# Decode attention in two parts: scores behind their head's recurrence, values one head later

## The chip, the cores and the metric

One NeuronCore of a Trainium2 chip runs the whole program. The metric is device time in microseconds (us), the median of several executions. Five engines work side by side: PE (TensorE, matmul), DVE (VectorE), ACT (ScalarE), POOL (GpSimd) and SP (SyncE, which here only issues loads and stores). Each runs its own list of instructions strictly in order and waits at an instruction until what it needs is there.

## What is computed

One layer of a hybrid decoder step, for a prompt of 1024 rows and for 8 sample rows that each bring one new token. Three branches (A attention, B spatial gating, C gated recurrence) read one projection of the normalised input, and one output projection merges them. The part that the change touches is branch A of the sample rows ("decode"): each sample row attends over its cache with three patterns of window and stride.

```python
PATTERNS = ((128, 1), (512, 4), (2048, 16))
def _dilated_step(q, k_new, v_new, k_buf, v_buf):
    kk = jnp.concatenate([k_buf, k_new], axis=1)
    vv = jnp.concatenate([v_buf, v_new], axis=1)
...
    for win, dil in PATTERNS:
        back = jnp.arange(win // dil + 1)[None, :] * dil
        idx = jnp.clip(W + t - back, 0, W + T - 1)
        s = jnp.einsum('bthe,btnhe->bthn', q, kk[:, idx])
        p, lse = _softmax_stats(s)
        outs.append(jnp.einsum('bthn,btnhe->bthe', p, vv[:, idx]))
        lses.append(lse)
    return _combine_patterns(outs, lses)
```

Branch C, in whose stage the decode work is placed, is per head a recurrence `S = exp(g) * S + k v`, `o = q S`, computed for the prompt in blocks of 128 rows and for each sample row as one step.

## The kernel before

The program runs branch A of the prompt, then hgrn() (branch C, from about 530 to 1065 us), then sgu() (branch B) and out_proj(). hgrn() goes over six heads in three pairs hp. For a pair c_proj_i projects the values, c_proj_z the output gates (both heads); for each head c_proj_qf projects q and f. All projections go through proj groups: weights are loaded raw by SP (load_w, line 190), ACT rounds them to the fast matmul type (line 192), POOL subtracts the rounded from the raw ones to get the low part (line 193), PE multiplies both parts, and DVE or ACT takes each finished group out of PSUM. There are two PSUM banks for these groups (tag "proj"), so PE can start a group only when the group before the last has been taken out. For q and the gates DVE does that (gate(), line 152, then a multiply in line 156).

c_head(h) is the recurrence of head h on the prompt: scans and exponentials (G, eG, H), then for four pairs of blocks the scaled copies T (lines 611 to 623, DVE), small matmuls lv and ls (PE), masked copies of lv into the block matrix cmat (lines 686 to 693, DVE), matmuls po from cmat, V, eG and the state S (PE), and the next state S (line 704, DVE). c_step(h) is the step of the 8 sample rows: two loads of state ss and two of values vb, six DVE operations of 128x512 (lines 735 to 737), eight matmuls pd.

decode(h) is the sample rows' attention for heads 2h and 2h+1 of branch A: POOL clears the score tile dsc; for each half of the batch a load of q (dqb), three loads of cached keys (dk), a multiply (line 913) and a reduce (line 914) for each; then the maximum over keys (917), across partitions by two transposes on PE (pmx, pmb) with a reduce and a copy between them (921, 922), the subtraction (925), Exp on ACT, a weighting (927), a sum (928), a matmul pdn and a reciprocal (931); then six loads of cached values (dv), 24 matmuls pda, a copy and two transposes (to_columns, pdt), and three small DVE operations (941, 942) that put the result into ysT, which only out_proj reads.

The decode tiles and c_step's vb and ss share one pool of five buffers (pq), used in turn; pd, pdt, pmx, pmb, pdn and pda share one PSUM bank (tag "tr"); dsc has one buffer. The order of each engine's instructions isn't written out: a scheduler (line 1058) fixes it when the program is built, by an estimate of its own of when each instruction could run, with ties and buffers in the order of the code. So where decode stands in the code decides where its instructions are mixed in among the others.

## Time and profile before

| | |
|---|---|
| median of 3 executions | 1364.37 us (1363.49 to 1366.2) |
| profiled execution, its own time | 1367.91 us |
| its span, first to last instruction | 1366.1 us |
| mean granted clock of PE | 0.951 |
| PE busy | 1277.9 us (94%) |
| DVE busy | 914.3 us (67%) |
| ACT busy | 661.0 us (48%) |
| POOL busy | 292.6 us (21%) |

The trace is of the profiled execution, so sums from it are held against 1367.91 us. A row of the timeline gives the start in us, the duration, the engine, the line, the operation with its tiles (result<-sources) and, in square brackets, how long the engine had been idle before it and which engine's result ended that. A row of busy time by stretch gives start:end, the length, the busy time of PE, PEld (weight load), DVE, ACT and POOL with the number of records, then the granted clock, the busy share of the DMA engines and GB/s. The granted clock (PEclk) is given as a share of full speed.

### The profile page before, as it was taken

The page shows a single profiled execution, that of the slowest core. Times are in us where ns is not written, and L with a number is a line of the kernel's source. Part 1 is how long each engine was busy: PE and PEld are TensorE (multiplying, and loading weights), DVE is VectorE, ACT ScalarE, POOL GpSimd, SP SyncE. Part 2 cuts the span into 40 slices and gives each one's busy share as a digit, 9 for nine tenths or more (in the row PEclk, how much of TensorE's full clock was granted, in tenths as well). Part 3 has the DMA queues.
Part 4 walks back from the last instruction along what each step waited for, and adds up shares of the span by engine and source line. Part 5 has one row for each costly group of instructions (what it writes and reads, how often), then busy time and mean ns, then how long its engine had stood idle before and what let it go on. Part 6 is the DMA issues. An engine that isn't in the chain of part 4 may idle for free. (4 is left out here: it accounts for less than half of the span.)

```text
span 1366.1 us, 27783 instructions
## 1 busy us (share of the span) xinstructions
PE 1277.9 (94%) x10634; PEld 1160.8 (85%) x10634; DVE 914.3 (67%) x2439; ACT 661.0 (48%) x1510; POOL 292.6 (21%) x267
## 2 busy tenths in 40 slices
PE   4799999999889999999999998998899999999999
PEld 3699798779779797898888888987788899899998
DVE  5835775565774656668888988888887623654653
ACT  4435454454443554456654744545544423544543
POOL 2531210131121212112202020211111135311221
PEclk9899899889999799999999999999999999999999
DMA  6241122220221212202433243434253313612210
GB/s 220 42 141 36 47 66 70 59 68 18 58 84 58 76 36 77 65 29 67 119 97 109 90 121 115 111 97 134 61 156 96 92 32 108 207 51 81 74 46 31
DMA packets 165044, 114.23 MB, mean 84 GB/s; under 512 B 13944, under 2 KB 158864, under 8 KB 164912
## 3 DMA queue, kind: packets, MB, share of 16 engines
q1 hardware_dynamic: 157520, 110.28, 27.3%
q10 hardware_dynamic: 6816, 1.54, 0.5%
q8 instruction: 83, 1.36, 0.4%
q0 software_dynamic: 576, 0.64, 0.3%
q14 instruction: 49, 0.40, 0.1%
HBM read 84.60 MB, written 22.09 MB: 78 GB/s over the span
## 5 line engine op out<-in xcount | busy, mean ns | idle before, releaser
L100 PE MATMUL pqk<-wh_qk,h 128*128 128x256 f32 x768 | 159.6, 299 | 5.2 <-ACT h L233 2.8
L100 PE MATMUL pc<-h,wh_cqf 128*128 128x344 f32 x576 | 144.1, 332 | 4.5 <-DVE cz L152 4.5
L100 PE MATMUL po<-woh,yl 128*128 128x256 f32 x512 | 145.0, 284 | 1.9 <-POOL yl L1011 1.9
L100 PE MATMUL po<-woh,yh 128*128 128x256 f32 x512 | 145.7, 285 | 0.0
L100 PE MATMUL po<-wol,yh 128*128 128x256 f32 x512 | 144.4, 282 | 0.0
L100 PEld LDWEIGHTS pqk<-wh_qk,h 128*128 128x128 f32 x768 | 131.5, 204 | 9.8 <-ACT h L233 3.0
L100 PE MATMUL pqk<-wl_qk,h 128*128 128x256 f32 x384 | 114.0, 297 | 0.0
L100 PEld LDWEIGHTS pc<-h,wh_cqf 128*128 128x128 f32 x576 | 102.1, 194 | 7.1 <-DVE cz L152 5.0
L100 PEld LDWEIGHTS po<-woh,yh 128*128 128x128 f32 x512 | 97.1, 190 | 5.6 <-ACT yh L1010 3.9
L100 PEld LDWEIGHTS po<-woh,yl 128*128 128x128 f32 x512 | 97.2, 190 | 4.1 <-POOL yl L1011 2.4
L100 PEld LDWEIGHTS po<-wol,yh 128*128 128x128 f32 x512 | 97.3, 190 | 0.0
L100 PE MATMUL pc<-h,wl_cqf 128*128 128x344 f32 x288 | 94.9, 332 | 2.5 <-POOL wl_cqf L193 2.2
L436 DVE CUSTOM_DVE_ANT_0 s<-s,masks 128x512 f32<-128x512 f32 (+2 forms) x144 | 77.7, 584 | 13.8 <-PE s L100 13.3
L100 PE MATMUL pi<-wh_ci,h 128*128 128x256 f32 x384 | 77.6, 297 | 4.8 <-DVE dsc L925 1.9
L100 PE MATMUL pv<-wh_v,h 128*128 128x256 f32 x384 | 79.1, 297 | 1.9 <-DVE ss L165 1.6
L473 ACT ACTIVATE st<-st 128x512 f32<-128x512 f32 (+2 forms) x84 | 44.2, 536 | 72.9 <-PE st L100 70.2
L100 PEld LDWEIGHTS pqk<-wl_qk,h 128*128 128x128 f32 x384 | 78.1, 204 | 0.5
L100 PE MATMUL pcz<-h,wh_cz 128*128 128x344 f32 x288 | 71.5, 326 | 0.3 <-DVE q L152 0.3
L100 PE MATMUL paz<-h,wh_az 128*128 128x344 f32 x288 | 71.1, 329 | 0.0
L100 PEld LDWEIGHTS pi<-wh_ci,h 128*128 128x128 f32 x384 | 64.2, 201 | 6.9 <-issue 2.9
L1011 DVE TENSOR_TENSOR yl<-yb,yh 128x512 fp32r<-128x512 f32 x44 | 30.4, 692 | 58.0 <-ACT yh L1010 58.0
L100 PEld LDWEIGHTS pv<-wh_v,h 128*128 128x128 f32 x384 | 65.7, 204 | 3.0 <-ACT yo L499 1.8
(376 smaller groups left out, 3665.1 us busy)
## 6 DMA issues: line engine op xcount, KB each, us to landing
wro<-in_w_out_dram SPq DMA_DIRECT2D x32, 256.0 KB
wr_qk<-in_w_in_dram SPq DMA_DIRECT2D x48, 128.0 KB
wr_cqf<-in_w_in_dram SPq DMA_DIRECT2D x48, 128.0 KB
dk<-in_cache_k_dram SPq DMA_DIRECT2D x24, 192.0 KB
dv<-in_cache_v_dram SPq DMA_DIRECT2D x24, 192.0 KB
xt<-in_x_prompt_dram SPq DMA_DIRECT2D x8, 512.0 KB
xr<-in_x_prompt_dram SPq DMA_DIRECT2D x32, 128.0 KB
out_o_yp_dram<-xr SPq DMA_DIRECT2D x32, 128.0 KB
```

What stands on the lines that cost most here:

```text
L100: nc.tensor.matmul(out, lhsT=lhsT, rhs=rhs, start=start, stop=stop)
L436: nc.vector.tensor_tensor_reduce(out=ps[:, :w], in0=ps[:, :w], in1=nmask[:, S - n + c:S - n + c + w], op0=ALU.add, op1=ALU.max, scale=1.0, ...
L473: nc.scalar.activation(st[:, :o], st[:, :o], AF.Exp)
L1011: (nc.gpsimd if piece == 0 else nc.vector).tensor_tensor(yl[:, sl, :], y, yh[:, sl, :].bitcast(F32), ALU.subtract)
```

## The change

decode(h) is cut in two functions. decode_scores(h) does everything up to the score tile: memsets, loads of q and keys, six multiplies and six reduces. decode_values(h) does the rest. decode_scores(h) stands where decode(h) stood, behind c_step(h). decode_values(h) stands one head later, between c_head(h+1) and c_step(h+1); that of the last head stands behind the loop. Two heads' scores are therefore alive at once: the even heads keep the tile dsc, the odd heads get columns 872 to 1009 of the 1024-column tile cmat, which nothing else uses.

```diff
--- before.py
+++ after.py
@@ -753,12 +753,16 @@
                 a = c_proj_qf(2 * hp)
                 Z = c_proj_z(hp)
                 c_head(2 * hp, *a, V[0], Z[0], At, lmask, dmask)
+                if hp:
+                    decode_values(2 * hp - 1, scw)
                 c_step(2 * hp, *a)
-                decode(2 * hp)
+                scw = decode_scores(2 * hp, None)
                 a = c_proj_qf(2 * hp + 1)
                 c_head(2 * hp + 1, *a, V[1], Z[1], At, lmask, dmask)
+                decode_values(2 * hp, scw)
                 c_step(2 * hp + 1, *a)
-                decode(2 * hp + 1)
+                scw = decode_scores(2 * hp + 1, cm[:, 872:1010])
+            decode_values(5, scw)
 
             n = HC * NS
             sq = pq("ssq", (P, n))
@@ -884,35 +888,38 @@
             cns[nm] = cp.tile(list(ins[nm].shape), F32, name=nm)
             tc.keep_in_program_order(nc.scalar.dma_start(cns[nm], ins[nm]))
 
-        def decode(p):
-
-            ROWS = ((P, 1920, 1), (96, 1536, 4), (96, 0, 16))
+        ROWS = ((P, 1920, 1), (96, 1536, 4), (96, 0, 16))
+
+        def rows(cache, new, p, bb, nm):
             ch = slice(p * P, (p + 1) * P)
-
-            def dk(nm, shape=(P, 4, P)):
-                return pq(nm, shape)
-
-            def rows(cache, new, bb, nm):
-                for kind, (n, r0, step) in enumerate(ROWS):
-                    t = dk(f"{nm}{p}_{bb}_{kind}")
-                    src = cache[0].rearrange("b r h e -> r b (h e)")[r0:r0 + n * step, 4 * bb:4 * bb + 4, ch]
-                    nc.sync.dma_start(t[0:n], src[0:n * step:step])
-                    if kind == 1:
-                        nc.sync.dma_start(t[n:n + 1], new[None, 4 * bb:4 * bb + 4, ch])
-                        n += 1
-                    yield kind, n, t
-
-            scw = small(f"dsc{p}", 138, bufs=1, tag="dsc").rearrange("p (k a) -> p k a", k=3)
+            for kind, (n, r0, step) in enumerate(ROWS):
+                t = pq(f"{nm}{p}_{bb}_{kind}", (P, 4, P))
+                src = cache[0].rearrange("b r h e -> r b (h e)")[r0:r0 + n * step, 4 * bb:4 * bb + 4, ch]
+                nc.sync.dma_start(t[0:n], src[0:n * step:step])
+                if kind == 1:
+                    nc.sync.dma_start(t[n:n + 1], new[None, 4 * bb:4 * bb + 4, ch])
+                    n += 1
+                yield kind, n, t
+
+        def decode_scores(p, home):
+
+            ch = slice(p * P, (p + 1) * P)
+            scw = small(f"dsc{p}", 138, bufs=1, tag="dsc") if home is None else home
+            scw = scw.rearrange("p (k a) -> p k a", k=3)
             sc = scw[:, :, 0:16]
             nc.gpsimd.memset(sc, NEG)
             nc.gpsimd.memset(scw[:, :, 16:], 0.0)
             for bb in range(2):
-                qb = dk(f"dqb{p}_{bb}")
+                qb = pq(f"dqb{p}_{bb}", (P, 4, P))
                 nc.sync.dma_start(qb, qkv_d[0, 4 * bb:4 * bb + 4, ch].partition_broadcast(P))
-                for kind, n, t in rows(ins["cache_k"], qkv_d[1], bb, "dk"):
+                for kind, n, t in rows(ins["cache_k"], qkv_d[1], p, bb, "dk"):
                     nc.vector.tensor_tensor(t[0:n], t[0:n], qb[0:n], ALU.mult)
                     nc.vector.tensor_reduce(sc[0:n, kind, 8 * bb:8 * bb + 8], t[0:n].rearrange("p b (h e) -> p (b h) e", e=E),
                                             AX.X, ALU.add)
+            return scw
+
+        def decode_values(p, scw):
+            sc = scw[:, :, 0:16]
             mx = small(f"dmx{p}", 32, bufs=1, tag="dmx")
             nc.vector.tensor_reduce(mx[:, 0:16], sc.rearrange("p k a -> p a k"), AX.X, ALU.max)
             pt = p_dk(f"pmx{p}")
@@ -931,7 +938,7 @@
             nc.vector.reciprocal(mx[:, 16:32], pd[:, 0:16])
             pa = p_dk(f"pda{p}")
             for bb in range(2):
-                for kind, n, t in rows(ins["cache_v"], qkv_d[2], bb, "dv"):
+                for kind, n, t in rows(ins["cache_v"], qkv_d[2], p, bb, "dv"):
                     for b in range(4):
                         mm(pa[32 * b:32 * b + 32, bb * P:(bb + 1) * P], scw[0:n, kind, 8 * bb + 2 * b:8 * bb + 2 * b + 32],
                            t[0:n, b, :], kind == 0, kind == 2)
```

No instruction is added or dropped; the scheduler orders them anew. The first heads' work up to about 700 us stays as it was. Three places show what moves. (Names carry head, half and group, then a number of the tile; x4 is four in a row.)

PE, the 24 value matmuls of head 1 (pda1). Before, they follow the recurrence of their own head (lv1, ls1), ahead of the second part of the gate projection pcz1_0_0:

```order
L100 MATMUL lv1_2_7940<-T1_2_q_7937,k1_7601 32x48 x4
L100 MATMUL ls1_2_7941<-V0_1_6397,kT1_0_7822 128x128
L100 MATMUL pda1_8279<-dv1_0_0_8280,dsc1_8230 32x128 x4
L100 MATMUL pda1_8279<-dv1_0_1_8286,dsc1_8230 32x128 x4
L100 MATMUL pda1_8279<-dv1_0_2_8293,dsc1_8230 32x128 x4
L100 MATMUL pda1_8279<-dv1_1_0_8299,dsc1_8230 32x128 x4
L100 MATMUL pda1_8279<-dv1_1_1_8305,dsc1_8230 32x128 x4
L100 MATMUL pcz1_0_0_8818<-h01_81,wh_cz1_2_8804 128x344
```

After, they stand in the middle of the projection of head 3's f (pc3_1_2) and read the scores from cmat:

```order
L100 MATMUL pc3_1_2_9559<-h00_80,wl_cqf3_1_9484 128x344
L100 MATMUL pda1_9365<-dv1_0_0_9366,cmat_6353 32x128 x2
L100 MATMUL po1_1_7953<-cmat_6353,V0_1_6397 128x128
L100 MATMUL pda1_9365<-dv1_0_0_9366,cmat_6353 32x128 x2
L100 MATMUL pda1_9365<-dv1_0_1_9372,cmat_6353 32x128 x3
L100 MATMUL po1_1_7953<-eG1_7730,S1_5_8038 128x128
L100 MATMUL po1_1_7953<-cmat_6353,V0_1_6397 128x128
L100 MATMUL po1_1_7953<-eG1_7730,S1_6_8120 128x128
L100 MATMUL pda1_9365<-dv1_0_1_9372,cmat_6353 32x128
L100 MATMUL pda1_9365<-dv1_0_2_9379,cmat_6353 32x128 x4
L100 MATMUL pda1_9365<-dv1_1_0_9385,cmat_6353 32x128 x4
L100 MATMUL pda1_9365<-dv1_1_1_9391,cmat_6353 32x128 x4
```

They have moved from before the gate projection of heads 2 and 3 to behind it. DVE, around the evacuation of the gate projection (cz1_0 and cz1_1, lines 152 and 156). Before, the operations of c_step(2) on vb2 and ss2 stand between the evacuations:

```order
L735 TENSOR_TENSOR vb2_1_9426<-vb2_1_9426,qs2_8787 128x512
L941 TENSOR_TENSOR dmx1_8263<-pdt1_8320,dmx1_8263 64x8 x2
L736 TENSOR_TENSOR ss2_1_9427<-ss2_1_9427,qs2_8787 128x512
L156 TENSOR_TENSOR cz1_0_8816<-cz1_0_8816,czt1_0_1_8874 128x344
L737 TENSOR_TENSOR ss2_0_9415<-ss2_0_9415,vb2_0_9414 128x512
L942 TENSOR_TENSOR ysT_73<-ysT_73,dmx1_8263 128x8
L152 TENSOR_SCALAR cz1_0_8816<-pcz1_0_2_8880 128x344
L737 TENSOR_TENSOR ss2_1_9427<-ss2_1_9427,vb2_1_9426 128x512
L704 SCALAR_TENSOR_TENSOR S1_3_7994<-S1_2_7990,eL1_7809,ls1_2_7941 128x128
L708 SCALAR_TENSOR_TENSOR cz0_1_6848<-po1_0_7824,gn_367,cz0_1_6848 128x512
L156 TENSOR_TENSOR cz1_0_8816<-cz1_0_8816,czt1_0_2_8905 128x344
L152 TENSOR_SCALAR cz1_1_8817<-pcz1_1_0_8911 128x344
```

After, the last evacuation, that of pcz1_1_2, stands among copies T2 of head 2's recurrence:

```order
L642 TENSOR_TENSOR eG2_8943<-eG2_8943,q2_8536 128x1024
L152 TENSOR_SCALAR cz1_1_8753<-pcz1_1_1_8878 128x344
L617 TENSOR_TENSOR T2_0_0_8975<-T2_0_0_8975,q2_8536 128x192
L617 TENSOR_TENSOR T2_0_1_8984<-T2_0_1_8984,q2_8536 128x192
L686 COPY_PREDICATED cmat_6353<-cmat_6353,lv1_4_7984 128x2x2x8
L686 COPY_PREDICATED cmat_6353<-cmat_6353,lv1_6_8070 128x2x8
L152 TENSOR_SCALAR cz1_1_8753<-pcz1_1_2_8909 128x344
L932 TENSOR_TENSOR cmat_6353<-cmat_6353,pmb1_9356 128x3x16
L618 TENSOR_TENSOR T2_0_0_8975<-T2_0_0_8975,dec2_0_0_8979 128x64
```

and c_step(2) follows some 55 rows later:

```order
L735 TENSOR_TENSOR vb2_0_9413<-vb2_0_9413,qs2_8723 128x512
L686 COPY_PREDICATED cmat_6353<-cmat_6353,lv2_0_9005 128x8x2
L736 TENSOR_TENSOR ss2_0_9414<-ss2_0_9414,qs2_8723 128x512
L564 SCALAR_TENSOR_TENSOR ft3_0_9588<-k3_9506,f3_9504 128x344
L564 SCALAR_TENSOR_TENSOR ft3_1_9591<-k3_9506,f3_9504 128x344
L686 COPY_PREDICATED cmat_6353<-cmat_6353,lv2_0_9005 128x2x8x2
L702 COPY S2_0_9054<-ls2_0_9006 128x128
L735 TENSOR_TENSOR vb2_1_9425<-vb2_1_9425,qs2_8723 128x512
L737 TENSOR_TENSOR ss2_0_9414<-ss2_0_9414,vb2_0_9413 128x512
L736 TENSOR_TENSOR ss2_1_9426<-ss2_1_9426,qs2_8723 128x512
```

The six operations of c_step(2) have moved from ahead of the three evacuations of cz1_1 to behind them. PE, the second half of head 2's recurrence (po2_1). Before, it stands behind 72 matmuls of head 4's f projection (pc4_1_0 to pc4_1_2):

```order
L100 MATMUL pc4_1_2_10623<-h01_81,wh_cqf4_3_10561 128x344
L100 MATMUL pc4_1_2_10623<-h11_83,wh_cqf4_3_10561 128x344
L100 MATMUL pc4_1_2_10623<-h01_81,wl_cqf4_3_10562 128x344
L100 MATMUL po2_1_9230<-cmat_6353,V1_0_8365 128x128
L100 MATMUL po2_1_9230<-eG2_9007,S2_3_9208 128x128
L100 MATMUL po2_1_9230<-cmat_6353,V1_0_8365 128x128
L100 MATMUL po2_1_9230<-eG2_9007,S2_4_9311 128x128
L919 MATMUL pmx3_10234<-ident_65,dmx3_10232 16x128
L100 MATMUL pc4_0_0_10661<-h00_80,wh_cqf4_0_10540 128x344
```

After, it stands inside the value projection (pi2_3) that comes ahead of that f projection:

```order
L100 MATMUL pi2_3_10424<-wl_ci2_2_10243,h01_81 128x256
L723 MATMUL pdt2_10161<-ident_65,pdt2s_10159 128x128 x2
L100 MATMUL pi2_3_10424<-wh_ci2_2_10242,h11_83 128x256
L100 MATMUL pi2_3_10424<-wh_ci2_2_10242,h01_81 128x256
L100 MATMUL pi2_3_10424<-wl_ci2_2_10243,h01_81 128x256
L100 MATMUL pi2_3_10424<-wh_ci2_2_10242,h11_83 128x256
L100 MATMUL po2_1_9166<-cmat_6353,V1_0_8301 128x128
L100 MATMUL po2_1_9166<-eG2_8943,S2_3_9144 128x128
L100 MATMUL po2_1_9166<-cmat_6353,V1_0_8301 128x128
L100 MATMUL po2_1_9166<-eG2_8943,S2_4_9247 128x128
L100 MATMUL pi2_3_10424<-wh_ci2_3_10248,h01_81 128x256
```

The recurrence's matmuls now come 72 projection matmuls of 344 columns and 30 of 256 earlier in PE's list.

## Rows read from the trace of the kernel before

**Rows 1.** The page, part 1: busy us (share of span) and instructions

```profile
PE 1277.9 (94%) x10634; PEld 1160.8 (85%) x10634; DVE 914.3 (67%) x2439; ACT 661.0 (48%) x1510; POOL 292.6 (21%) x267
```

**Rows 2.** Busy time by stretch, start:end us, length, engines, PEclk, DMA

```profile
760.00:880.00 120.00, 113.17 (x1185) 105.05 (x1184) 105.05 (x314) 62.81 (x148) 20.83 (x18) 0.97 0.39 109
...
sum 420.00, PE 392.67 PEld 357.18 DVE 360.25 ACT 222.08 POOL 74.67; mean PE 98.17 PEld 89.30 DVE 90.06 ACT 55.52 POOL 18.67
```

**Rows 3.** Timeline of PE, matmuls with idle time before them

```profile
791.81 0.76 PE L100 MATMUL pc<-h,wh_cqf 128*128 128x344 f32 x2 [1.95 <-DVE cz L152]
...
822.89 0.39 PE L100 MATMUL pi<-wh_ci,h 128*128 128x256 f32 x1 [1.61 <-DVE q L152]
...
832.09 0.37 PE L100 MATMUL pdn<-dmx,ones 128*128 128x16 f32 x2 [2.44 <-DVE eL L640]
...
906.18 0.43 PE L100 MATMUL pd<-ss,qs 128*32 128x128 f32 x8 [1.45 <-DVE ss L737]
...
938.71 0.86 PE L100 MATMUL pc<-h,wh_cqf 128*128 128x344 f32 x2 [2.58 <-DVE cz L152]
...
966.72 1.05 PE L100 MATMUL pss_bv<-wr_bv,hs 128*8 128x256 f32 x16 [1.77 <-DVE q L152]
...
970.90 0.55 PE L100 MATMUL pbv<-wh_bv,h 128*128 128x256 f32 x1 [3.14 <-DVE dsc L925]
...
1010.54 0.80 PE L100 MATMUL po<-cmat,V 128*128 128x128 f32 x2 [2.20 <-DVE cmat L693]
```

**Rows 4.** Busy time by stretch, ahead of and behind gaps

```profile
783.00:791.70 8.70, 6.24 (x47) 5.02 (x45) 8.70 (x16) 4.58 (x11) 7.29 (x5) 1.00 0.33 87
791.80:795.20 3.40, 3.39 (x12) 3.39 (x13) 2.88 (x16) 1.66 (x6) 0.00 (x0) 0.54 1.06 263
832.00:836.00 4.00, 3.91 (x22) 3.94 (x23) 3.97 (x19) 0.65 (x3) 0.00 (x0) 0.63 0.02 6
938.70:942.00 3.30, 3.29 (x12) 3.29 (x13) 3.20 (x6) 0.93 (x3) 0.00 (x0) 0.52 0.78 236
970.90:976.00 5.10, 5.10 (x24) 5.10 (x25) 4.97 (x23) 4.60 (x12) 0.00 (x0) 0.50 0.24 78
1010.50:1013.50 3.00, 2.96 (x14) 2.96 (x15) 2.94 (x10) 0.00 (x0) 0.00 (x0) 0.50 0.85 276
```

**Rows 5.** Timeline of POOL in two bursts of subtractions

```profile
783.67 4.71 POOL L193 TENSOR_TENSOR wl_cqf<-wr_cqf,wh_cqf 128x512 fp32r<-128x512 f32 x2 [22.25 <-ACT wh_cqf L192]
...
788.38 2.58 POOL L193 TENSOR_TENSOR wl_cqf<-wr_cqf,wh_cqf 128x512 fp32r<-128x512 f32 x2
...
962.59 6.33 POOL L193 TENSOR_TENSOR wl_bv<-wr_bv,wh_bv 128x512 fp32r<-128x512 f32 x4 [26.51 <-ACT wh_bv L192]
```

**Rows 6.** Timeline of DVE beside those bursts and behind one

```profile
788.63 1.19 DVE L618 TENSOR_TENSOR T<-T,dec 128x64 f32<-128x64 f32 x1
789.74 1.59 DVE L156 TENSOR_TENSOR cz<-cz,czt 128x344 f32<-128x344 f32 x1
...
791.76 0.21 DVE L618 TENSOR_TENSOR T<-T,dec 128x64 f32<-128x64 f32 x1
...
967.80 2.21 DVE L566 SCALAR_TENSOR_TENSOR k<-k,lb,f 128x1032 f32<-128x1032 f32 x1
```

**Rows 7.** Timeline of DVE in a full stretch

```profile
845.53 0.69 DVE L735 TENSOR_TENSOR vb<-vb,qs 128x512 f32<-128x512 f32 x1
846.14 0.68 DVE L737 TENSOR_TENSOR ss<-ss,vb 128x512 f32<-128x512 f32 x1
```

**Rows 8.** Busy time by stretch, instructions of tile pc alone

```profile
857.00:872.20 15.20, 11.92 (x72) 11.31 (x72) 0.00 (x0) 0.91 (x2) 1.00 0.67 185
```

**Rows 9.** Timelines of DVE and PE, masked copy and first matmul of po2_1

```profile
870.00 0.37 DVE L693 COPY_PREDICATED cmat<-cmat,lv 96x192 f32<-96x192 uint16 x1
...
872.09 0.38 PE L100 MATMUL po<-cmat,V 128*128 128x128 f32 x2
```

**Rows 10.** Waits of POOL: engine line waited for, us, times, longest

```profile
POOL dsc L907 <- PE pda L100: 59.8, 3, 21.3
```

## The prediction

> **What bounds the kernel now.** I read the profile's page first, for which engine is busy, then the busy times by stretch, then the gaps ahead of TensorE's (PE's) instructions, then what VectorE (DVE) and GpSimd (POOL) did just ahead of each gap. PE is busy 94% of the span and DVE 67% [rows 1]. The change only touches the recurrence stage, and the order of PE's instructions first differs at about 700 us. From 640 to 1060 us PE is busy 392.67 of 420 us, so 27.3 us of idle time are all that a new order can win directly; DVE is busy 360.25 of the same 420, and 105.05 of the 120 us from 760 to 880 [rows 2]. DVE is not full, yet nearly always late by a little.
>
> The gaps show that. Eight that the new order can reach are 1.95, 1.61, 2.44, 1.45, 2.58, 1.77, 3.14 and 2.20 us, 17.1 us together, and each ends on a DVE result: the evacuation of a projection bank (line 152), the copy of eL (line 640), ss (737), the decode subtraction (925), the masked copy into cmat (693) [rows 3]. A gap costs twice: ahead of the 1.95 us gap the granted clock is 1.00, the 2.4 GHz level; in the stretches behind the five gaps of 1.95, 2.44, 2.58, 3.14 (with 1.77 just ahead of it) and 2.20 us it averages 0.54, 0.63, 0.52, 0.50 and 0.50, where 0.50 is the 1.2 GHz level [rows 4]. Full speed less these, times their lengths, is 1.6 + 1.5 + 1.6 + 2.6 + 1.5 = 8.7 us.
>
> Why DVE is late stands one engine further. POOL subtracts the rounded weights from the raw ones in bursts of four (line 193): two instructions from 783.67 and two from 788.38, then four from 962.59 on [rows 5]. Inside them a DVE multiply of 128x64 elements takes 1.19 us, and an add-sized one of 128x344 takes 1.59 us; the same 128x64 multiply takes 0.21 us once the burst is over, and k of head 5 takes 2.21 us [rows 6]. All of these read two tiles from SBUF. The evacuation that PE waits for sits behind such an instruction.
>
> The Trainium skill has the rule, in SBUF — State Buffer, section "Who interferes with whom": a DVE instruction with two SBUF inputs and a GpSimd instruction that reads SBUF share a pair of ports, which whichever starts first holds to its end. The trace agrees (1.19 against 0.21 us for one shape). By that rule the bursts stay as costly as they are wherever the decode steps stand, which is my second rival.
>
> **The change, part by part.** Nothing is added or taken away: the same mults, reduces, matmuls and loads run. So the sum is about who stands ahead of whom. At each gap I compare what no longer stands ahead on DVE (that much earlier is the awaited result) with what no longer stands ahead on PE (that much earlier does PE ask for it); the difference is the slack won. In a full stretch one 128x512 DVE instruction follows another after about 0.61 us, although each is recorded with 0.68 or 0.69 [rows 7], so I use 0.6.
>
> *Values one head later.* The reductions, transposes, exponential and 24 value matmuls of head h now stand behind c_head(h+1), and c_step(h+1) behind them. At the 1.95 us gap (head 3's second bank waits for the last evacuation of cz1_1), the six operations of c_step(2) (6 x 0.6 = 3.6 us), the multiply cz1_1 (1.5) and one of T2 (1.1), and ten small ones of decode 1 (0.12 to 0.17 each, 1.3) are now behind the evacuation: 7.5 us. PE loses 24 value matmuls (1.6 us), pd2's eight (0.9), and five small ones (0.7): 3.2 us. Slack won: 4.3, more than the gap. Part of the 7.5 ran ahead of moments in which DVE waited anyway; if only cz1_1 and T2 count (2.6), against the PE work that stood behind them (pd2 and its transposes, 1.3), it is 1.3, and 0.65 us of gap stays. I take the whole 1.95. The same count gives at the next gaps, in us of slack: head 2's pi2_0 +1.5 (gap 1.61, removes 1.47), pdn2 +3.2 (2.44), pd4 +11.7 (1.45; it simply stands later), pc5_1_1 +2.4 (DVE 4.7 for six operations of c_step(4) and small ones, less PE 2.3; removes 2.42 of 2.58), pss_bv0 and pbv0 +4.5 and +2.9 (the slow k5 and decode 4's steps now stand behind q5's evacuations; of 1.77 + 3.14 I count 3.03, since a delay of the first is part of the second), po4_1 +2.6 (2.20). Sum: 1.95 + 1.47 + 2.44 + 1.45 + 2.42 + 3.03 + 2.20 = **15.0 us of gaps**, and up to 8.7 of clock behind them.
>
> *Where slack is lost.* Second half of head 2's recurrence, po2_1, at 872.09 us: it waits for a masked copy that started at 870.00 and took 0.37, so it has 1.72 us to spare [rows 9]. Ahead of it PE now lacks 72 matmuls pc4 (11.9 us in their window [rows 8]), 30 of pi2 (3.7), pd3 and its transposes (1.0): 16.6 us less cover. DVE lacks there the six mults and six reduces of decode 3 (12 x 0.6 = 7.2) and c_step(3) (3.8), 0.4 of small ones: 11.4. So 16.6 - 11.4 - 1.7 = **3.5 us of new wait**, which by the pattern of [rows 4] brings some 1.5 us of half clock. A little later pcz2_0_0 waits for q4 behind 13.6 us more of head 3's recurrence; its 8.7 of slack becomes -3.3, the same lag and not paid twice.
>
> *What the saved time meets.* 5.9 us of the gaps (1.95 + 1.47 + 2.44) lie ahead of that place. If PE comes there 5.9 earlier and DVE no earlier, they are lost again. DVE idles 15 us of 760 to 880 [rows 2], mostly waiting for PE, and these shrink as PE hurries: I let half come through and charge 3.0.
>
> *Bursts on other work.* With the same bursts beside other DVE work, new small gaps open where now none are. I have no row of it; the bounds are 0 and the 15.0 that the present order pays, and I take 4.0, near the low end, because the evacuations gain 2 to 4 us of slack against multiplies stretched by about 1 us each.
>
> *Second home for scores.* Scores of heads 1, 3 and 5 go to unused columns of the mask tile, so POOL's memset need not wait for the value matmuls of the head before; in before that wait was 59.8 us in three waits [rows 10]. POOL's next subtraction waits over 20 us for ScalarE's cast anyway [rows 5], so I price it at nothing; if a subtraction did queue behind a late memset it would cost what a late lo-weight costs PE, one gap of 1.5 to 2 us.
>
> *Loads.* The key and value loads share five buffers in the same cyclic order; SP now issues weights for the coming projections ahead of c_step's and decode's loads. Only one place is tighter: the last value tile of head 3 is issued behind two weight loads and a store, and PE has 3.5 us of other work between the first and the last value matmul instead of 5.6. Bound 0 to 1 us; I take 0.
>
> **Sum.** Won 15.0 + half of 8.7 (4.3, because a stretch behind a removed gap may have a smaller one left in it) = 19.3. Lost 3.5 + 1.5 + 3.0 + 4.0 = 12.0. Net **7 us faster**. The profiled execution took 1367.91 us, 3.5 above the median of 1364.37; taken off the median, 1364.4 - 7 = **1357.4 us**.
>
> **Rivals.** *Slower: DVE's lag at head 2 to 3 decides.* For it: the 11.4 us of cover on DVE against 16.6 on PE are counted instruction by instruction, and from 760 to 1000 DVE is the engine that PE nearly always waits for. If DVE has no idle time to give back there, the 5.9 us won ahead of po2_1 come back as waits, and the 9.1 behind it too, since 13.6 us of recurrence now stand ahead of q4 and then of the banks of head 5. What is left is 3.5 + 1.5 = 5 us slower: **1369.4**. It decides as soon as DVE's idle time between 846 and 872 us cannot take up 3.5 us. Against it: the slack at the later gaps is counted too, and is positive.
>
> *No change: the gaps belong to the bursts.* POOL's bursts stay, each stretches four or so DVE instructions by about 1 us, and whichever evacuation stands behind is late: eight gaps are moved, not removed. Then the 15.0 come back elsewhere, with their clock, and the result is **1364.4 within 2.7**. For it: the gaps at 791.81, 966.72 and 970.90 of [rows 3] stand at the end of a burst or right behind one [rows 5]. Against it: what PE waits for is not the burst but the queue of DVE work ahead of the evacuation, and that queue gets 2 to 4 us shorter.
>
> *The gain is larger.* If the lag at po2_1 is covered (0) and all of the clock comes back, 15.0 + 8.7 - 4.0 - 3.0 = 16.7: **1347.7**.
>
> **How the numbers follow.** 0.2% of 1364 us, 2.7 us, is about what a measurement of this kernel can tell from no change. Chances: net gain as summed 0.42, the larger gain 0.13, bursts decide 0.23, DVE's lag decides 0.22. The first two are faster by over 0.2% except for a tail of the first; some of the bursts' case spills over to faster: faster 0.56, same 0.21, slower 0.23. The range goes from the larger gain to the slower rival's 1369.4: 1347.5 to 1369.5.
>
> **What would show it.** Right: no gap over 1 us ahead of pc of heads 3 and 5, pdn2 and pbv0; PE's idle time in the stage falls from 27 to about 18 us; a new wait of po2_1 on cmat of 2 to 4 us. Wrong: PE's idle time stays at 27 us with other names in the list; or the wait at po2_1 exceeds 5 us and banks of heads 4 and 5 wait for q; or PE waits for dv tiles (loads), which I priced at nothing.

## The result: slower, and where the time went

The changed kernel takes 1379.70 us against 1363.93 of the kernel before (medians of four executions each): a ratio of 1.0103, 95% interval 1.0085 to 1.0121. That is slower, and beyond the upper end of the predicted range (1369.5). The profiled executions stand 13.0 us apart in span, 1379.1 against 1366.1 us; the traces below account for these 13.0, not for the 15.8 of the medians.

The page's first part, of the kernel after (busy us, share of the span, instructions), beside [rows 1]:

```profile
PE 1278.9 (93%) x10634; PEld 1164.7 (84%) x10634; DVE 918.9 (67%) x2439; ACT 662.7 (48%) x1510; POOL 298.2 (22%) x267
```

PE is busy 1.0 us longer than before, over the whole program. So nearly all of the 13.0 us is time in which PE does nothing. Busy time by stretch (columns as in [rows 2]) tells where. First the kernel after, then the kernel before; the last row of each is the whole stage in which the order of PE's instructions differs:

```profile
690.00:790.00 100.00, 91.56 (x1074) 85.76 (x1072) 85.67 (x261) 55.36 (x134) 17.91 (x15) 0.98 0.29 83
790.00:850.00 60.00, 47.79 (x464) 43.24 (x463) 50.02 (x154) 26.95 (x64) 7.03 (x8) 0.87 0.39 113
850.00:960.00 110.00, 104.62 (x1121) 96.00 (x1120) 79.75 (x249) 57.43 (x139) 22.13 (x17) 0.96 0.35 98
960.00:1100.00 140.00, 127.25 (x1450) 114.42 (x1449) 116.56 (x366) 62.55 (x150) 24.05 (x14) 0.96 0.37 105
...
680.00:1100.00 420.00, 379.35 (x4221) 346.08 (x4221) 341.96 (x1048) 210.84 (x506) 76.13 (x56) 0.96 0.35 99
```

```profile
690.00:790.00 100.00, 95.33 (x1140) 87.05 (x1138) 89.58 (x274) 55.59 (x135) 17.60 (x18) 1.00 0.35 98
790.00:850.00 60.00, 54.04 (x528) 50.55 (x529) 50.95 (x153) 26.95 (x65) 6.48 (x7) 0.94 0.41 115
850.00:960.00 110.00, 102.63 (x1175) 93.75 (x1177) 94.84 (x272) 61.45 (x148) 19.86 (x15) 0.98 0.39 113
960.00:1100.00 140.00, 132.28 (x1407) 119.69 (x1398) 103.31 (x341) 57.45 (x141) 24.92 (x20) 0.96 0.34 99
...
680.00:1100.00 420.00, 392.42 (x4355) 357.79 (x4355) 348.56 (x1062) 209.78 (x505) 72.58 (x62) 0.98 0.37 105
```

420 less 379.35 is 40.65 us of idle PE, 420 less 392.42 is 27.58: 13.07 more, which is the difference of the spans. I call this number the stage's idle time below. From 790 to 850 us PE does 464 matmuls where it did 528, at a granted clock of 0.87 where it had 0.94. The length less PE's busy time, after less before, is the idle time added in each stretch: 3.8 us from 690 to 790, 6.3 from 790 to 850, 2.0 less to 960, and 5.0 more to 1100. Matching the same matmul in both traces points at the same place: the first matmul of the group pc3_1_2 (about 799 us) comes 0.9 us later than before, that of pc3_0_2 11 us, that of pi2_0 11.7, that of pi2_1 14.4. Behind that the lag goes up and down with the two orders, between 7 and 24 us at the first matmuls of the groups. **Of the 13.1 us more idle time, 10.0 arise up to 850 us, between head 1 and head 2.** Behind it the new order wins and loses, 3.0 us in sum.

PE's waits from 690 to 1100 us in the kernel after (waited for, us in total, times, longest):

```profile
PE pbv L100 <- ACT qt L155: 5.8, 1, 5.8
PE pi L100 <- DVE q L152: 5.6, 1, 5.6
PE pi L100 <- DVE sd_ci L260: 4.8, 1, 4.8
PE pc L100 <- DVE cz L152: 4.3, 1, 4.3
...
PE pda L100 <- DMA dv<-in_cache_v_dram: 3.5, 2, 2.6
```

The timeline has them one by one; these answer to [rows 3]:

```profile
789.46 0.55 PE L100 MATMUL pc<-h,wh_cqf 128*128 128x344 f32 x2 [4.33 <-DVE cz L152]
...
834.60 0.55 PE L100 MATMUL pi<-wh_ci,h 128*128 128x256 f32 x1 [5.61 <-DVE q L152]
...
846.70 0.55 PE L100 MATMUL pi<-wh_ci,h 128*128 128x256 f32 x1 [4.77 <-DVE sd_ci L260]
...
949.63 0.43 PE L100 MATMUL pda<-dv,cmat 96*32 96x128 f32 x8 [2.65 <-DMA dv<-in_cache_v_dram]
...
987.08 0.55 PE L100 MATMUL pbv<-wh_bv,h 128*128 128x256 f32 x1 [5.81 <-ACT qt L155]
```

The gap of 1.95 us at pc3_1_1 is now 4.33 us one group earlier (pc3_1_0). The 1.61 us at pi2_0 are 5.61, and behind it stands a gap that before had not: 4.77 us at pi2_1. The 1.77 and 3.14 us at the head of branch B are one gap of 5.81. Four gaps of [rows 3] are gone, as predicted: pdn2 (2.44), pd4 (1.45), pc5_1_1 (2.58), po4_1 (2.20), 8.7 us together. Other gaps are new or longer: the 2.65 us at the values of head 3, 2.89 us at 738 us (po, 1.42 before) and 1.99 us at 1062 us (pbz).

Right ahead of the evacuation that ends the 4.33 us no work of the sample rows stands. It is that of pcz1_1_1, which ran at 781.85 us before. It now stands behind operations of head 2's recurrence, which run inside a burst of subtractions (783.48 to 790.02); one of them, eG2 (line 642), took 1.23 us before:

```profile
785.46 1.24 DVE L623 TENSOR_TENSOR T_q<-f,q 128x128 f32<-128x128 f32 x1
786.61 2.28 DVE L642 TENSOR_TENSOR eG<-eG,q 128x1024 f32<-128x1024 f32 x1
788.81 0.50 DVE L152 TENSOR_SCALAR cz<-pcz 128x344 f32<-128x344 f32 x1
```

Why pi2_0 waits 5.61 us is read on DVE. Its bank becomes free when q of head 3 has been evacuated (line 152, at 833.96). VectorE's timeline of the kernel after, just ahead of that:

```profile
825.36 1.19 DVE L617 TENSOR_TENSOR T<-T,q 128x192 f32<-128x192 f32 x1
827.49 0.75 DVE L916 TENSOR_TENSOR dk<-dk,dqb 128x512 f32<-128x512 f32 x1 [0.95 <-DMA dk<-in_cache_k_dram]
828.16 2.29 DVE L566 SCALAR_TENSOR_TENSOR k<-k,lb,f 128x1032 f32<-128x1032 f32 x1
830.38 0.25 DVE L686 COPY_PREDICATED cmat<-cmat,lv 128x48 f32<-128x48 uint16 x1
830.49 1.18 DVE L618 TENSOR_TENSOR T<-T,dec 128x64 f32<-128x64 f32 x1
831.59 0.68 DVE L916 TENSOR_TENSOR dk<-dk,dqb 97x512 f32<-97x512 f32 x1
...
832.76 0.68 DVE L916 TENSOR_TENSOR dk<-dk,dqb 96x512 f32<-96x512 f32 x1
833.36 0.67 DVE L917 TENSOR_REDUCE dsc<-dk 128x8 f32<-128x512 f32 x1
833.96 0.50 DVE L152 TENSOR_SCALAR q<-pc 128x344 f32<-128x344 f32 x1
```

The rows of lines 916 and 917 are the scores of head 2 (line 913 and 914 before). Their twelve operations ran from 794 to 805 us in the kernel before; here they run from 827 to 846, in the middle of the evacuations. The 2.29 us of k, the 1.19 and the 1.18 us stand inside one of POOL's bursts of subtractions (824.94 to 831.59), as those of [rows 6] do. The other eight operations of the scores stand ahead of the third addition into sd_ci (line 260, at 846.15), for which pi2_1 waits.

And the stretch that the scores have left is empty. Busy time by stretch, kernel after, then before:

```profile
797.00:809.00 12.00, 12.00 (x152) 10.25 (x154) 3.62 (x11) 3.01 (x6) 0.00 (x0) 1.00 0.31 89
812.00:847.00 35.00, 22.79 (x225) 20.19 (x225) 33.85 (x90) 17.02 (x39) 6.76 (x5) 0.87 0.48 136
```

```profile
797.00:809.00 12.00, 12.00 (x80) 12.00 (x79) 11.05 (x32) 3.87 (x7) 0.00 (x0) 1.00 0.54 153
812.00:847.00 35.00, 30.86 (x386) 27.92 (x385) 29.52 (x94) 19.70 (x48) 5.52 (x6) 0.95 0.28 85
```

From 797 to 809 us DVE works 3.62 us where it worked 11.05, while PE is busy all 12 us in both. From 812 to 847 DVE is full, 33.85 of 35 us, and PE works 22.79 where it worked 30.86. What DVE waits for in the empty stretch is the recurrence of head 1, which runs through PE, DVE and ACT in turn, and at its end the exponentials of head 3's f (k, line 555); the two longest waits of its timeline in the kernel after:

```profile
803.11 0.35 DVE L704 SCALAR_TENSOR_TENSOR S<-S,eL,ls 128x128 f32<-128x128 f32 x1 [2.81 <-PE po L100]
...
807.59 0.70 DVE L558 TENSOR_SCALAR k<-k 128x1032 f32<-128x1032 f32 x1 [2.65 <-ACT k L555]
```

Before, the sample step and the scores of head 2 filled such waits. Their loads come late too: SP issues those of head 2's sample step from 804.10 us on (756.37 before), with waits of 11.7 and 3.9 us for head 1's value matmuls (pda), and those of its keys from 822.31 (788.25 before). The clock adds to it; the 1.0 us by which PE is busy longer is all of it that shows in the sum. Stretches of the kernel after, right behind the gaps of 4.33 and 4.77 us:

```profile
789.40:793.00 3.60, 3.54 (x14) 3.57 (x15) 3.60 (x19) 2.79 (x9) 0.62 (x1) 0.57 0.44 130
...
846.70:850.00 3.30, 3.30 (x15) 3.30 (x16) 3.30 (x9) 1.20 (x3) 0.00 (x0) 0.50 0.46 131
```

### The profile page after: what moved, and what is told of

Same layout as the page of the kernel before. It is cut to its first block, busy times and chain, and to the rows that moved or that the text cites. A ratio compares the mean times of both kernels' runs of the same rounds, so it can differ in the third digit from the quotient of the medians.

```text
span 1379.1 us, 27779 instructions
## 1 busy us (share of the span) xinstructions
PE 1278.9 (93%) x10634; PEld 1164.7 (84%) x10634; DVE 918.9 (67%) x2439; ACT 662.7 (48%) x1510; POOL 298.2 (22%) x267
## 4 chain that ended last, share of the span: by engine, by line
PE 67%; DVE 17%; DMA 5%; issue 5%; ACT 4%; POOL 1%; SPq 1%; DVEq 0%; POOLq 0%; ACTq 0%
PE po L100 14%; PE pv L100 9%; PE pqk L100 9%; PE paz L100 5%; PE pc L100 5%; PE st L100 4%; PE pbu L100 3%; PE pbz L100 3%; PE pi L100 3%; DMA dk<-in_cache_k_dram 3%; PE pcz L100 2%; PE s L100 2%; PE pb L100 2%; PE pbv L100 1%; DVE T L611 1%
## 5 line engine op out<-in xcount | busy, mean ns | idle before, releaser
L100 PE MATMUL pqk<-wh_qk,h 128*128 128x256 f32 x768 | 156.7, 296 | 5.5 <-DVE ss L164 3.5
L100 PE MATMUL pi<-wh_ci,h 128*128 128x256 f32 x384 | 80.4, 302 | 13.0 <-DVE q L152 5.6
```

The lines of the kernel that those rows point to most:

```text
L100: nc.tensor.matmul(out, lhsT=lhsT, rhs=rhs, start=start, stop=stop)
```

## The experiments

The expectations give theories letters as they came up; each says what its own means. Two means were used. In the six kernels from home_only to behind_all the places of the calls in the code are changed, and the scheduler orders everything anew. In those below them the order of a kernel is held: a table of places says which instruction follows which on each engine, and a dependency that adds no wait ties each to the one ahead of it; single rows of the table can then be moved. before_fewkeys holds the order of before, and takes as long as before. The stage's idle time is that of the profiled execution, 27.6 us in before; it doesn't give the time alone. cstep_first idles 36.0 us and takes about as long as before, with PE busy 1266.3 us instead of 1277.9. The profiled execution of late_not1 took 1362.61 us, 5 us over its median.

| kernel | median us | ratio to before, 95% interval | stage's idle time, us |
|---|---|---|---|
| after | 1379.70 | 1.0103 (1.0085 to 1.0121) | 40.7 |
| home_only | 1356.66 | 0.9941 (0.9920 to 0.9962) | 25.0 |
| late_1 | 1372.94 | 1.0062 (1.0038 to 1.0086) | 34.4 |
| late_not1 | 1357.64 | 0.9957 (0.9940 to 0.9975) | 26.7 |
| cstep_first | 1366.14 | 1.0017 (0.9998 to 1.0036) | 36.0 |
| late_1_behind | 1375.50 | 1.0075 (1.0053 to 1.0097) | 35.5 |
| behind_all | 1373.91 | 1.0061 (1.0046 to 1.0077) | 41.8 |
| after_fewkeys | 1375.44 | 1.0065 (1.0038 to 1.0092) | 36.3 |
| before_fewkeys | 1364.70 | 0.9994 (0.9976 to 1.0012) | 25.8 |
| after_nolow | 1348.58 | 0.9881 (0.9854 to 0.9907) | 20.0 |
| before_nolow | 1332.29 | 0.9749 (0.9726 to 0.9771) | 6.3 |
| after_hoist2 | 1376.12 | 1.0070 (1.0048 to 1.0091) | 38.9 |
| home_hoist | 1349.96 | 0.9887 (0.9854 to 0.9919) | 20.4 |
| late_1_back | 1371.79 | 1.0060 (1.0039 to 1.0081) | 36.5 |
| late_1_back2 | 1367.79 | 1.0022 (1.0007 to 1.0037) | 33.5 |
| late_1_back3 | 1360.09 | 0.9974 (0.9963 to 0.9985) | 26.1 |

### Which part, and which head

These kernels share one loop. LATE names the heads whose values come one head later: none in home_only, as here; head 1 in late_1; all but head 1 in late_not1.

```diff
+            LATE = ()
+            late = []
...
+                    c_head(h, *a, V[j], Z[j], At, lmask, dmask)
+                    if late:
+                        decode_values(*late.pop())
+                    c_step(h, *a)
+                    scw = decode_scores(h, cm[:, 872:1010] if j else None)
+                    if h in LATE:
+                        late.append((h, scw))
+                    else:
+                        decode_values(h, scw)
```

The second home of the scores alone:

> The second home for the scores of odd heads alone: values right behind the scores, as before the change. Theory A (the loss comes from where the decode work of one head stands between 800 and 847 us, not from the home): PE's order stays that of before for the first 6500 instructions, so the time is that of before, within 4 us (ratio 0.997 to 1.003). Theory B (scores in the mask tile cost something by themselves, on POOL or by sharing a tile): 5 to 15 us slower than before. Theory C (any new order of the scheduler scatters by about 1%): anything between 0.99 and 1.01.

It is faster by 0.6%, which neither A nor B had; only the wide range of C holds it. Its order is that of before up to about 1000 us. Its lead over before is 0.3 us until pcz2_0_0, then grows by 1.2 us at pcz2_1_0 (914 us), 1.0 by pbv0_3 (997 us) and 1.2 by pbv1_3 (1032 us), where the 2.20 us wait of po4_1 for cmat in [rows 3] is 0.15 us, with one of 1.31 us for S; the rest of the 12.0 us between the spans of the two profiled executions comes behind that, where PE's orders differ (the one of before is 4 us over its median). Through which step the second home does that was not taken apart. For the question here it settles one thing: the second home isn't what makes the change slow, and against it the late values cost 23 us.

Head 1's values late, and all but head 1's:

> Only head 1's values stand one head later; all other heads' values right behind their scores. Theory A: the whole loss is made where head 1's values were pushed behind head 2's recurrence (in the trace after, 13.5 of the 15 us by which the stage is late arise between 800 and 847 us), so this alone is 9 to 16 us slower than before (ratio 1.007 to 1.012). Theory B: half the time of the change at most, since only the homes count. Theory C: no relation to the loss of the full change; a value near 1.00 is as likely.

> All heads' values one head later except head 1's, which stay right behind its scores. Theory A: the loss of the full change is not made; 0 to 5 us slower than before (ratio 1.000 to 1.004), because the later heads in the trace after gained as much as they lost. If instead each late head costs its share, about 11 us slower (four of five). Theory C: anything between 0.99 and 1.01.

Busy time by stretch from 790 to 850 us, late_1 and then late_not1:

```profile
790.00:850.00 60.00, 49.55 (x461) 45.02 (x461) 49.42 (x154) 27.51 (x65) 7.26 (x8) 0.87 0.41 114
```

```profile
790.00:850.00 60.00, 56.29 (x670) 52.15 (x671) 54.74 (x161) 32.58 (x80) 9.91 (x10) 0.97 0.41 116
```

Head 1 makes most of the loss. With its values late, the three gaps of after are back (4.34, 4.78 and 3.83 us) and the clock is 0.87; with the five others late there is no gap over 1 us at pi2_0 or pi2_1, one of 3.00 us at head 3's bank, the clock is 0.97, and the time is that of home_only within 1 us. late_1 lies at the low edge of theory A's range, late_not1 below its range. Against home_only, head 1 alone costs 16.3 of the 23.0 us of the full change, the five others alone 1.0; the 5.8 us that all cost together beyond these were not taken apart.

### The order of the calls

cstep_first puts the sample step ahead of the values, with all heads late:

```diff
                     c_head(h, *a, V[j], Z[j], At, lmask, dmask)
+                    c_step(h, *a)
                     if late:
                         decode_values(*late.pop())
-                    c_step(h, *a)
```

late_1_behind (head 1 late) and behind_all (all heads) put the values behind both:

```diff
                     c_step(h, *a)
                     scw = decode_scores(h, cm[:, 872:1010] if j else None)
+                    if late:
+                        decode_values(*late.pop())
```

> As the change, but c_step(h+1) stands ahead of decode_values(h) in the code, so that its loads and six DVE operations don't wait for the five tile buffers that the value tiles hold. Theory A: the six operations of c_step(2) (3.7 us from start to start) leave the full stretch of DVE between 812 and 846 us, the twelve key operations of head 2 stay in it: half of the loss is gone, 5 to 10 us slower than before. Theory B and C: as the change, 10 to 16 us slower, or unrelated.

> Head 1's values late again, all others at once, but in the code they stand behind c_step(2) and decode_scores(2) instead of ahead of them. The five tile buffers are handed out in the order of the code, so head 2's state, value and key tiles no longer wait for head 1's value tiles: on DVE vb2 stands at row 1171 and the first dk2 at 1242 (1326 and 1368 with the values ahead, 1235 and 1296 in before). Theory E (what was late is not head 1's values but head 2's sample step and scores, which queue for the buffers behind them and so fall into the stretch where DVE is full): the loss of late_1 is gone, 1354 to 1362 (ratio 0.992 to 0.999). Theory F (head 1's own value work, 24 matmuls and some fifteen small operations, costs that much in its new place): 1370 to 1376 as late_1.

> The same for all heads: decode_values(h) behind decode_scores(h+1). Theory E: none of the heads pushes the next one's scores back; 1350 to 1364 (ratio 0.990 to 1.000), against 1379.7 with the values ahead. Theory F: 1370 to 1385.

With c_step first, 13.6 of the 15.8 us come back, more than the half expected, though the scores of head 2 stay late (826 us on) and a gap of 6.37 us opens elsewhere (694 us, pd1). late_1_behind was to tell whether the ring of five buffers, whose order follows the code, is the cause. There c_step(2) runs from 746 to 753 us and the scores of head 2 from 772 to 790, earlier even than before, and PE waits 5.36 us at pi2_0 all the same, 4.85 us at ls (758 us, ahead of the scores) and 2.52 at head 3's bank. So theory E missed, the ring alone isn't it, and earlier isn't better either. The time is the one that theory F named, but late_1_back below speaks against F. What makes this order slow was not settled. behind_all, where theory E missed too, has 8.18 us at pi2_0.

### What stands ahead of the evacuation

after_fewkeys and before_fewkeys hold their orders and let the twelve operations of head 2's scores work on 64 of 512 columns:

```diff
-                    nc.vector.tensor_tensor(t[0:n], t[0:n], qb[0:n], ALU.mult)
+                    w = slice(0, 1) if p == 2 else slice(0, 4)
+                    e = slice(0, E) if p == 2 else slice(0, P)
+                    x = t[0:n, w, e]
+                    nc.vector.tensor_tensor(x, x, qb[0:n, w, e], ALU.mult)
```

> The changed kernel in its own order, but head 2's twelve key operations (dk2) work on 64 of their 512 columns; most of head 2's scores are left out. Each falls from 0.6 to about 0.1 us, 6 us of DVE work less between 827 and 846 us. Theory A: DVE is full there and PE waits for what stands behind, so 5 to 9 us below the changed kernel (ratio to before 1.004 to 1.008). Theory D: DVE waits for the key tiles' loads instead; under 2 us.

> The kernel before in its own order with the same part of head 2's scores left out. Its twelve key operations stand between 794 and 806 us, where PE does not wait behind them at once. Theory A: 0 to 3 us below before (ratio 0.998 to 1.0). If DVE's whole amount of work is what counts, wherever it stands, it gains the same 5 to 9 us as the changed kernel does.

The same work costs 4.3 us at its new place (1379.70 to 1375.44, a little under the 5 to 9 expected) and nothing at its old one (1364.70 beside 1364.68 of before). The gaps at pi2_0 and pi2_1 shrink to 3.8 and 2.1 us; they don't go. Still there are k, the scans and the loads of the keys; what each of them costs was not tested.

after_hoist2 holds the order of after and moves eight evacuations (two of cz, three of q3, three additions into sd_ci) up in DVE's list, to where their source is ready:

```diff
+L152 TENSOR_SCALAR q_9505<-pc_0_2_9659 128x344
 L916 TENSOR_TENSOR dk_0_0_9448<-dk_0_0_9448,dqb_0_9446 128x512
 L566 SCALAR_TENSOR_TENSOR k_9506<-k_9506,lb_370,f_9504 128x1032
...
+L260 TENSOR_TENSOR sd_ci_10263<-pss_ci_10254,sd_ci_10263 8x256
 L917 TENSOR_REDUCE dsc_9443<-dk_0_0_9448 128x8
-L152 TENSOR_SCALAR q_9505<-pc_0_2_9659 128x344
```

> The changed kernel with every engine's order held as it was, but for eight DVE instructions of heads 1 to 3: the evacuations of pcz1_1_1, pcz1_1_2, pc3_0_0, pc3_0_1, pc3_0_2 and three additions to sd_ci2 stand 2 to 8 us earlier, where their matmuls have just ended. Theory A (PE's three waits of 4.33, 5.61 and 4.77 us come from evacuations that stand in DVE's list behind the decode and c_step work which the change moved there): those 14.7 us fall to under 5, and the time is 8 to 15 us below the changed kernel's 1379.7 (ratio to before 0.998 to 1.006). Theory D (the work itself is late, because loads wait for tile buffers, and PE's waits would only pass to the next result): less than 4 us gained.

3.6 us instead of the 8 to 15 that I expected. The gaps at 789 and 834 us go, and one of 8.28 us takes their place at pi2_1: with DVE full from 812 to 847 us, what is moved up moves other work down. The expectation put all three gaps down to decode and sample steps; for the one at 789 us that was wrong, as shown above.

### The bursts

The rival that the bursts decide can be priced. The low parts of the weights of branch C and of v in branch B are cleared (a memset writes, and reads nothing) instead of subtracted, in the held orders of both kernels; PE multiplies zeros in as many matmuls.

```diff
-                nc.gpsimd.tensor_tensor(lo, raw, hi.bitcast(F32), ALU.subtract)
+                if nm[:2] in ("cq", "ci", "cz", "bv"):
+                    nc.gpsimd.memset(lo.bitcast(F32), 0.0)
+                else:
+                    nc.gpsimd.tensor_tensor(lo, raw, hi.bitcast(F32), ALU.subtract)
```

> The changed kernel in its own order, but POOL clears the low parts of the weights of branches B's v and C instead of subtracting; the low parts are left out of the products. POOL then reads nothing from SBUF in its bursts. Rival of the prediction (waits follow the bursts): DVE's two-input operations are no longer stretched, 10 to 25 us faster than the changed kernel, and most of its distance to before vanishes with the bursts. Theory E: both kernels gain, the changed one not over 5 us more than before.

> The kernel before in its own order with the same low parts cleared instead of subtracted. If the bursts cause its eight waits, these shrink and it gains 10 to 20 us (ratio 0.985 to 0.993). If the waits are only late DVE work as such, under 5 us.

Both win about the same, 31.1 us (after) and 32.7 us (before), more than the 10 to 25 and 10 to 20 expected, and stay 16.3 us apart, as far as with the bursts (15.8). The clearing differs in more than what it reads: a memset of wl_cqf takes 528 ns on average where the subtraction took 1592, and it waits for no cast by ACT. So how much of the 31 to 33 us is the stretching alone isn't shown. The page's first part, before_nolow, beside [rows 1]:

```profile
PE 1263.7 (95%) x10634; PEld 1152.0 (87%) x10634; DVE 876.8 (66%) x2439; ACT 660.4 (50%) x1510; POOL 241.6 (18%) x267
```

DVE's instructions are the same 2439, and take 37.5 us less; PE is busy 14.2 us less, at a mean granted clock of 0.959 instead of 0.951, and the stage's idle time is 6.3 us. The multiply of 128x64 elements in c_head (line 618, 621 in before_nolow) shows the stretching go; durations in ns are the shortest, the median and the longest of 72, in before and then in before_nolow:

```profile
L618 DVE TENSOR_TENSOR T<-T,dec x72: 202/215/1278, 669.2 to 1036.6; 128x64 f32<-128x64 f32 x72
```

```profile
L621 DVE TENSOR_TENSOR T<-T,dec x72: 203/216/245, 665.7 to 1001.6; 128x64 f32<-128x64 f32 x72
```

The median stays, the longest falls from 1278 to 245 ns. In before six of the 72 overlap a subtraction, and four of these take 494 to 1278 ns; in before_nolow seven overlap a memset and take 204 to 224 ns. In after_nolow the two gaps of the loss are still there, on PE's timeline:

```profile
814.36 0.55 PE L100 MATMUL pi<-wh_ci,h 128*128 128x256 f32 x1 [3.42 <-DVE q L152]
...
826.50 0.40 PE L100 MATMUL pi<-wh_ci,h 128*128 128x256 f32 x1 [3.77 <-DVE sd_ci L263]
```

So the subtractions are dear, but they are not what tells the two kernels apart.

### Putting the work back, one piece after the other

Three kernels hold late_1's order and put sample work of heads 1 and 2 back to where home_only has it, on all engines that run it: first the values of head 1 (late_1_back), then the sample step of head 2 as well (late_1_back2), then the twelve operations of head 2's scores as well (late_1_back3). Of DVE's list, the last of the three steps:

```diff
+L921 TENSOR_TENSOR dk_0_0_9448<-dk_0_0_9448,dqb_0_9446 128x512
 L686 COPY_PREDICATED cmat<-cmat,lv_6_8133 128x2x8x2
...
+L922 TENSOR_REDUCE dsc_9443<-dk_1_1_9467 97x8
 L708 SCALAR_TENSOR_TENSOR cz_1_6848<-po_1_8016,gn,cz_1_6848 128x512
+L922 TENSOR_REDUCE dsc_9443<-dk_1_2_9472 96x8
...
-L921 TENSOR_TENSOR dk_0_0_9448<-dk_0_0_9448,dqb_0_9446 128x512
 L566 SCALAR_TENSOR_TENSOR k_9569<-k_9569,lb_370,f_9567 128x1032
```

> The kernel late_1 (only head 1's values late, 1372.9 us) with its order held on every engine, but the value work of head 1 alone (29 matmuls and transposes, 10 DVE and 2 ACT operations, 8 loads) put back to the times it has in the kernel with the second home alone (1356.7 us). Theory F (the late value work itself costs the time): 1355 to 1362, ratio to before 0.994 to 0.999. Theory G (the scheduler, given the other order of the code, has sorted everything else anew: head 2's recurrence earlier, its sample step and scores elsewhere, and that order is the slower one): 1368 to 1375, ratio 1.003 to 1.008.

> As late_1_back (order of late_1 held, value work of head 1 put back), and head 2's sample step too: six DVE operations, eight matmuls pd2 and what follows them, with their loads, at the times of the kernel with the second home alone. Theory H (DVE is full between 812 and 846 us because the sample step and the scores of head 2 landed there): 3.7 us of DVE work leave that stretch, 1362 to 1368. Theory G (the recurrence of head 2 and the projections of head 3 were sorted anew, and that is the slow part): 1368 to 1375.

> The same, and head 2's twelve key operations with their loads are put back too, so that all decode work of heads 1 and 2 up to the scores stands where it stood in the kernel with the second home alone; recurrence, projections and evacuations keep the order of late_1. Theory H: 1355 to 1362. Theory G: 1368 to 1375.

The values themselves are not the cause: put back, they change 1372.94 to 1371.79, less than the intervals. The sample step gives 4.0 us (to 1367.79), the scores 7.7 more (to 1360.09), in this order of putting back; the scores alone were not put back. Together that is 11.7 of the 15.1 us between late_1_back and home_only, and both times lie in theory H's ranges, the first at the edge. Busy time from 790 to 850 us, late_1_back and then late_1_back3:

```profile
790.00:850.00 60.00, 44.51 (x407) 41.23 (x408) 51.62 (x149) 27.70 (x64) 10.82 (x10) 0.85 0.43 122
```

```profile
790.00:850.00 60.00, 55.44 (x624) 51.14 (x624) 54.51 (x167) 33.99 (x82) 8.05 (x8) 0.94 0.33 88
```

DVE does more in the same 60 us (54.51 against 51.62), and PE 10.9 us more. The gap at pi2_0 falls from 5.52 to 3.44 us, that at pi2_1 (4.69) is gone. The 3.4 us that stay (1360.09 against 1356.66) belong to the rest that the scheduler re-sorted; the gap at head 3's bank is still 3.98 us there (791 us). They were not taken apart.

### A faster version

home_hoist keeps the values with their head and only the second home, holds home_only's order, and moves 29 evacuations up in DVE's list (one of them shown):

```diff
+L152 TENSOR_SCALAR cz_0_8815<-pcz_0_2_8879 128x344
 L737 TENSOR_TENSOR ss_0_9414<-ss_0_9414,vb_0_9413 128x512
 L954 TENSOR_TENSOR ysT<-ysT,dmx_8262 128x8
-L152 TENSOR_SCALAR cz_0_8815<-pcz_0_2_8879 128x344
```

> The kernel with the second home alone (1356.7), its order held, with 29 evacuations between 690 and 1080 us moved up DVE's list to where their matmuls have just ended. Theory A: the waits of 1.96, 1.62, 2.26, 1.76 and 2.85 us on evacuations shrink to under 1 each; 4 to 10 us below 1356.7 (ratio to before 0.988 to 0.993). Theory D: what is pushed back is the recurrence, so the waits on cmat and S grow by as much; within 3 us of 1356.7.

1349.96 us, a ratio of 0.9887 (0.9854 to 0.9919), the fastest of those that leave nothing out; 6.7 us of it come from the 29 moves, as theory A had it. In after_hoist2 eight moves of the same kind gave 3.6.

## Why the prediction was wrong

**The step that failed** is the counting of slack under "Values one head later". For each gap I took what no longer stands ahead on DVE less what no longer stands ahead on PE, from the start of the stage. That counts work, as if DVE had been busy throughout. At pi2_0 the count gave +1.5 us; the gap grew by 4.0 us. Busy time from the program's start to the evacuation that pi2_0 waits for, before and then after:

```profile
0.00:822.35 822.35, 757.43 (x5732) 678.59 (x5732) 566.86 (x1458) 413.70 (x910) 171.74 (x175) 0.93 0.27 77
```

```profile
0.00:833.96 833.96, 761.02 (x5740) 682.13 (x5740) 568.48 (x1475) 418.03 (x921) 174.26 (x178) 0.93 0.26 75
```

As a sum of work the count is nearly right: ahead of that place PE is busy 3.6 us longer than before and DVE 1.6 us, which is 2.0 us of slack. But DVE's idle time ahead of it has grown from 255.5 to 265.5 us. It now idles where the removed work had filled waits: 3.62 of 12 us busy where it was 11.05 (797 to 809 us), and then the work comes due at once. A moved operation costs its duration at its new place and gives back nothing at its old one if DVE only waits there for something else. The prediction's own caution at the 1.95 us gap ("part of the 7.5 ran ahead of moments in which DVE waited anyway") was this very effect, and was carried no further than that gap. At that gap the count also looked only at what leaves from ahead of one evacuation, that of pcz1_1_2: the wait moved to the one before it, which the new order puts behind head 2's eG2 and copies T2 (788.81 us instead of 781.85).

**The order of the code, taken for a detail.** The text said that c_step(h+1) now stands behind the values, and counted its operations against single gaps. That it comes 49 us later (from 763.9 to 812.5), that the scores of head 2 follow 34 to 40 us later than before, and where both land, stood in no term. By late_1_back3 they are 11.7 us, the scores 7.7 of them.

**The checks that it named.** No gap over 1 us ahead of pdn2 and of pc of head 5: right. Ahead of pc of head 3 and of pbv0: wrong, 4.33 and 5.81 us. The stage's idle time was to fall from 27 to about 18 us; it rose to 40.7. The new wait of po2_1 on cmat (3.5 us, with 1.5 of clock) did not come. Of the signs of being wrong two came near: a bank waits 5.61 us for q of head 3, where heads 4 and 5 were named, and pbv0 starts at 987.08, when q of head 5 has left its bank (986.94; the row names ACT's qt, which ended just behind it); and PE waits 2.65 us at the values of head 3 for a load, which was priced at 0 to 1.

**The slower rival** had the mechanism, DVE's lag, the sign, and nearly the region, but its place (po2_1, 872 us) is 25 to 38 us behind the true one, and its price of 5 us is a third of what was measured. It let the lag arise from less cover on PE; at pi2_0 and pi2_1 it arises from work that DVE does too late. That its sign was right is in part luck.

**The rival of the bursts** is half right: clearing instead of subtracting wins 31 to 33 us in each kernel, more than the 27.6 us of idle time that I set out to win. But it forecast no change, and the difference between the kernels stays without the subtractions. The Trainium skill (SBUF — State Buffer, section "Who interferes with whom") says that a DVE instruction with two SBUF inputs contends with a GpSimd instruction that reads SBUF, and not with one that only writes it. The traces agree: the multiply of 128x64 takes up to 1278 ns beside a subtraction and at most 224 beside a memset.

**The second home**, priced at nothing, is worth 7 us by home_only. Through which wait isn't shown. It does not take the waits of [rows 10] away: of their 59.8 us POOL still waits 44.7 there (38.5 for dsc and 6.2 for cmat, from 690 to 1100 us).

## What to carry to other kernels

Before moving filler work out of the way of a critical result, look at what the engine would do at the old place: where it waits for other engines the filler was free, and at the new place it has its full price. Count slack with the engine's idle time in, by the busy share of the stretch left and of the stretch entered (here 11 of 12 us, and 29.5 of 35 already before the work came). Where a scheduler orders by the place in the code, move one step at a time: the late values of five heads alone cost 1 us and those of one 16 of the 23, mostly through the next head's sample step and scores.

## What was not expected of the hardware

POOL's subtractions are busy for few of the stage's microseconds (72.58 of 420 for all of POOL), and the stretched DVE instructions of [rows 6] lose about 1 us each. Yet clearing instead of subtracting took 37.5 us off DVE's recorded work and 32.7 us off the program (1364.95 to 1332.29): nearly as many on the path that sets the end as off DVE, an engine that is busy 67% of the span. POOL's shorter and earlier work may be part of it.
